# Earlier release of the projection weight pool, two more gate-row buffers, and output weights on ScalarE's DMA queue, in a hybrid Fourier and state-space layer

## The chip, the core and the metric

The kernel runs on one core of one Trainium2 chip, in one launch. The metric is the time of that launch in device microseconds (us). A core has a matrix engine (TensorE, PE in the profile; PEld is its loading of weights), a vector engine (VectorE, DVE), a scalar engine (ScalarE, ACT), a general engine (GpSimd, POOL), and SyncE (SP), which here only issues DMAs. Each engine executes its instructions in the order in which they were written for it, and waits at an instruction until the semaphores that it names are reached.

## The reference, cut to what matters

One layer works on 2048 latent tokens and 256 context tokens of width 1024, all in fp32:

```
u, zf, zs, xbc, dt_raw = split(h @ w_in)       # h: modulated, normalised tokens
mixed = real(fft2(u)) over (2048 positions, 64 channels of a group)
four  = (mixed @ w_fourier + b_fourier) * silu(zf)          # 512 channels
xbc   = silu(depthwise_conv3x3(xbc) + b)                    # x 1536, B 512, C 512
y     = ssd_scan_forward(...) + ssd_scan_backward(...) + d_skip * x
ssd   = group_rmsnorm(y * silu(zs)) * norm_w                # 1536 channels
out   = final_rmsnorm(x + gate * (concat(four, ssd) @ w_out))
```

The scan works in 16 chunks of 128 positions (and 2 of context), 4 groups of 6 heads, in both directions.

## The kernel before, in words

Matrix products are made in three passes over a high and a low part of each operand (`hh`/`hl` are the high and low part of the tokens, `wh`/`wl` those of a weight tile; L176, L177 and L178 are the three passes of a projection). The stages are, by the profile: normalisation, the `u` projection and the first DFT; the projection and convolution of 20 channel tiles; then the backward scan, interleaved with the `zs` projection (the gate) of token blocks 0 to 2; then the `zs` projection of token block 3, interleaved with the rest of the Fourier branch; then 64 output units of one chunk and group each, which read everything back from DRAM.

**Projection weights.** `weights` (L163) fills a tile in a chain: one DMA of 512 KB to the single buffer `raw` (SP's queue), a copy to `wh` on ACT (L68), and the subtraction that gives `wl` on POOL (L72). `raw` can be loaded again when `wl` is done. `wh` and `wl` have two buffers each. The pool that holds them is `p1w`; it is closed after the first two units' first step (L1090).

**The `zs` block 3 and the Fourier branch.** `interleave` (L756) writes twelve tiles of the projection (tiles 19 to 8, of 24 matmuls each) and puts the steps of a side list between them by their estimated cost: `f_table` (L905; PE at L909), `f_step2` (L916; PE at L923), `f_extra` (L982), and `f_mm` (L962; PE at L941 to L943). `f_mm` is called for four channel tiles `dt`, two halves of the positions `h` and two parts `i`; each call has 12 matmuls. After its second part `f_gate` (L945) adds the bias, and multiplies into the gate rows `zf` (L960), which `zf_load` (L896) has fetched, 1 MB for each `dt`. After the second half of a `dt` the product is stored to DRAM (`fm_d<-zf`). There are two `zf` buffers, so the third and fourth `dt` wait at `zf_load` for the store of the first and second. `interleave` hands back what did not fit (`left`), which is written behind the projection (L1043).

**The units.** Step `s1` of a unit loads its rows `rt`, `lt` (small), `cb`, `chl`, `yb`, `zs`, `xg`, `bt`. PE makes the arguments of the decay (L1079), DVE masks them (L1081), ACT takes the exponential (L1083), PE multiplies (L1115 to L1117, L1136 to L1138, L1151, L1154), the norm follows (L1167), and the output product (L1210 to L1212) reads the output weights `wo`.

**The output weights.** They are 32 pieces of 512 KB (`hl<-wo_d`, `hh<-wo_d`), which `w_load` (L853) puts into the places of the tokens as these come free, in four groups of 8 loads. Group 1 is written in the side list before the last `f_mm` calls, group 0 behind the last projection tile (L1042), and groups 2 and 3 in the units 0 and 1 behind `issue_after`, which holds a group until named instructions have gone.

**What sets the order.** The program is written for all engines together; a scheduler then simulates it and fixes one order for each engine. Every DMA of this kernel is issued on SP's queue. The DMAs take eight semaphores in turn, and a DMA is only issued when the DMA before it on its semaphore has landed.

Of the kernel before, what the change touches and what calls it, by code (L numbers as in the profile page):

```python
# [9 lines left out]
F32 = mybir.dt.float32  # L10
# [8 lines left out]
P = 128  # L19
# [30 lines left out]
def mixer_layer(ctx: ExitStack, tc: tile.TileContext, A: dict, out: bass.AP, taps=None):  # L50
# [798 lines left out]
    wos = {}  # L849
# [3 lines left out]
    def w_load(n):  # L853
        r, k = 2 * (n % 4), worder[n]
        wos[k] = tuple(t[:, r:r + 2, c:c + 512] for t, c in wplace[n // 4])
        for i in range(2):
            load(wos[k][i].bitcast(F32), wo_d[k, :, i].rearrange("p (a b) -> p a b", a=2).bitcast(F32))
# [7 lines left out]
    fa = pool("fa", 2, stack=pfa)  # L865
    fb = pool("fb", 2, stack=pfb, side="right")
    c64 = [const_tile("c64", where=fa), const_tile("s64", where=fa)]
# [4 lines left out]
    fo = {"new": main_psum}  # L872
    gls = {}
# [22 lines left out]
    def zf_load(dt):  # L896
        def go():
            zf = zft[dt] = fb.tile([P, 16, P], F32, name="zf", tag="zf")
            load(zf[:].rearrange("p a b -> p (a b)"), zfT_d[dt])
            if dt != 2:  # L900
                nc.scalar.activation(zf, zf, AF.Silu)
            nc.gpsimd.tensor_tensor(out=zf[:, :, 64], in0=zf[:, :, 64], in1=ye[:, dt], op=ALU.mult)
        return go
# [41 lines left out]
    def f_gate(dt, p0, p1, parts):  # L945
        zf = zft[dt]
        q32 = fb.tile([P, 512], F32, name="q32", tag="q32", bufs=1)
        copy(q32, p1)
# [59 lines left out]
    dts = [0, 3, 1, 2]  # L1008
# [8 lines left out]
    fmm = [(dt, h) for dt in dts[:2] for h in range(2)] + [(dt, h) for h in range(2) for dt in dts[2:]]  # L1017
    for n, (dt, h) in enumerate(fmm):
        if n in (4, 5):
            side.append((0.0, zf_load(dt)))  # L1020
        if n == 6:
            side.append((0.0, lambda: w_group(1)))
        side += [(2.6, f_mm(dt, h, i)) for i in range(2)]
    left = interleave(zs_ops([(i, (3,)) for i in range(19, 7, -1)]), side, 10, .75)
# [16 lines left out]

    w_group(0)  # L1042
    for _, fn in left:  # L1043
        fn()
# [45 lines left out]
    p1w.close()  # L1090
# [157 lines left out]
    for u in range(NU + 2):  # L1248
        if u + 1 < NU:
            if u > 0:  # L1250
                s1(u + 1)
            s2(u + 1)
        if u < 2:
            with tc.issue_after(fo["st"]), tc.issue_after(units[u + 1]["ld"]):
                w_group(u + 2)
        if u < NU:
            s3(u)
            s4(u)
        if 1 <= u <= NU:
            s5(u - 1)  # L1260
        if u >= 2:
            s6(u - 2)
# [110 lines left out]
```

## Time and profile before

| what | value |
| --- | --- |
| median of 3 runs | 1911.37 us (1909.71 to 1916.48) |
| the profiled execution | 1912.61 us |
| its span from the first to the last instruction | 1910.8 us |
| mean granted TensorE clock | 0.977 of full speed |
| PE busy | 1809.4 us, 95% of the span |
| DVE, ACT, POOL busy | 66%, 46%, 47% |
| data moved by DMA | 301.80 MB, 158 GB/s in the mean |

A row of the timeline gives the start and the length of an instruction, its engine and line, what it writes and reads, and in brackets how long the engine stood idle before it and what released it. The chain of waits is followed back from the last instruction; each row is one piece of it. A row of the windows gives the busy time and the number of instructions of PE, PEld, DVE, ACT and POOL in a stretch of time, then the granted TensorE clock, the busy share of the DMA engines, and the GB/s moved. An issue on SP's queue is written `SPq`; its length is that of the issue, not of the transfer.

### The profile page before, as it was taken

The page shows a single profiled execution, that of the slowest core. Times are in us where ns is not written, and L with a number is a line of the kernel's source. Part 1 is how long each engine was busy: PE and PEld are TensorE (multiplying, and loading weights), DVE is VectorE, ACT ScalarE, POOL GpSimd, SP SyncE. Part 2 cuts the span into 40 slices and gives each one's busy share as a digit, 9 for nine tenths or more (in the row PEclk, how much of TensorE's full clock was granted, in tenths as well). Part 3 has the DMA queues.
Part 4 walks back from the last instruction along what each step waited for, and adds up shares of the span by engine and source line. Part 5 has one row for each costly group of instructions (what it writes and reads, how often), then busy time and mean ns, then how long its engine had stood idle before and what let it go on. Part 6 is the DMA issues. An engine that isn't in the chain of part 4 may idle for free.

```text
span 1910.8 us, 28132 instructions
## 1 busy us (share of the span) xinstructions
PE 1809.4 (95%) x9142; PEld 1492.4 (78%) x9142; DVE 1258.5 (66%) x1809; ACT 873.9 (46%) x1968; POOL 906.2 (47%) x791
## 2 busy tenths in 40 slices
PE   6989999999999999989999999957999999999997
PEld 2779988888888888878888877845778777777776
DVE  3744569788888897557665622334677777667865
ACT  3632235445445455346666653223444444435443
POOL 1320034224123134178787732145777777668742
PEclk8999999999999999999999999977999999999999
DMA  7432344535445345367776774786445444444441
GB/s 256 166 93 77 90 131 151 171 113 166 138 130 160 122 129 174 120 200 217 213 218 206 216 247 136 224 287 218 125 143 151 130 132 134 147 124 138 144 137 44
DMA packets 291332, 301.80 MB, mean 158 GB/s; under 512 B 34098, under 2 KB 242066, under 8 KB 290675
## 3 DMA queue, kind: packets, MB, share of 16 engines
q1 hardware_dynamic: 291186, 300.01, 50.6%
q8 instruction: 73, 1.20, 0.3%
q14 instruction: 73, 0.59, 0.1%
HBM read 196.82 MB, written 103.10 MB: 157 GB/s over the span
## 4 chain that ended last, share of the span: by engine, by line
PE 75%; DMA 9%; DVE 5%; POOL 5%; issue 3%; ACT 2%; SPq 1%; POOLq 0%; DVEq 0%; ACTq 0%
PE pj L178 11%; PE pj L177 11%; PE pj L176 11%; PE po L1212 6%; PE po L1210 6%; PE po L1211 6%; PE py L1151 2%; PE parg L1079 2%; POOL sl L72 2%; PE pj L508 1%; PE pj L509 1%; PE pj L510 1%; PE py L1154 1%; DMA ev<-in_wout 1%; PE ptr L569 1%
## 5 line engine op out<-in xcount | busy, mean ns | idle before, releaser
L178 PE MATMUL pj<-hh,wl 128*128 128x512 f32 x1152 | 452.6, 393 | 0.8 <-POOL wl L72 0.8
L177 PE MATMUL pj<-hl,wh 128*128 128x512 f32 x1152 | 452.1, 392 | 0.0
L176 PE MATMUL pj<-hh,wh 128*128 128x512 f32 x1152 | 450.0, 394 | 2.1 <-ACT img L68 1.6
L636 DVE SCALAR_TENSOR_TENSOR pacc<-img,c_convw,pacc 128x1024 f32<-128x1024 f32 x320 | 410.0, 1287 | 58.5 <-ACT pacc L633 49.2
L72 POOL TENSOR_TENSOR wl<-raw,wh 128x1024 fp32r<-128x1024 f32 x48 | 116.5, 2428 | 345.4 <-ACT wh L68 294.8
L178 PEld LDWEIGHTS pj<-hh,wl 128*128 128x128 f32 x1152 | 216.4, 188 | 47.4 <-POOL wl L72 1.4
L176 PEld LDWEIGHTS pj<-hh,wh 128*128 128x128 f32 x1152 | 217.0, 188 | 44.4 <-ACT img L68 2.3
L177 PEld LDWEIGHTS pj<-hl,wh 128*128 128x128 f32 x1152 | 216.6, 188 | 40.9 <-issue 1.8
L807 ACT ACTIVATE xd<-xt,smb 128x64 f32<-128x64 f32 x384 | 100.8, 336 | 80.2 <-POOL yb L811 78.5
L1210 PE MATMUL po<-hl,mh 128*128 128x512 f32 x288 | 117.5, 408 | 0.7 <-ACT mh L68 0.4
L1211 PE MATMUL po<-hh,mh 128*128 128x512 f32 x288 | 114.8, 399 | 0.0
L1081 DVE COPY_PREDICATED parg<-msk,parg 128x384 f32<-128x384 uint8 x128 | 71.1, 556 | 64.1 <-PE parg L1079 63.7
L1212 PE MATMUL po<-hl,ml 128*128 128x512 f32 x288 | 109.8, 401 | 2.6 <-POOL ml L72 2.4
L1083 ACT ACTIVATE w<-parg 128x384 f32<-128x384 f32 x128 | 62.3, 486 | 104.8 <-DVE parg L1081 104.5
L72 DVE TENSOR_TENSOR xl<-xw,xh 128x384 fp32r<-128x384 f32 x76 | 63.7, 843 | 59.3 <-ACT xh L68 57.9
L1120 POOL TENSOR_TENSOR ts<-ts,yb 128x384 f32<-128x384 f32 x64 | 73.6, 1150 | 57.6 <-issue 27.2
L1079 PE MATMUL parg<-rt,lt 128*128 128x384 f32 x256 | 88.0, 372 | 11.2 <-DMA rt<-cum_d 4.1
L72 POOL TENSOR_TENSOR ml<-gt,mh 128x384 fp32r<-128x384 f32 x64 | 68.4, 1068 | 58.8 <-ACT mh L68 55.4
L68 ACT ACTIVATE xh<-xw 128x384 fp32r<-128x384 f32 x136 | 69.9, 516 | 55.2 <-PE pst L1138 14.9
L1084 DVE TENSOR_TENSOR w<-w,cb 128x768 f32<-128x768 f32 x64 | 81.6, 1275 | 12.1 <-ACT w L1083 10.9
L72 DVE TENSOR_TENSOR sl<-hbk,sh 128x384 fp32r<-128x384 f32 x64 | 59.9, 937 | 38.4 <-ACT sh L68 38.2
L72 POOL TENSOR_TENSOR sl<-ev,sh 128x512 fp32r<-128x512 f32 x32 | 42.1, 1317 | 89.1 <-DMA wo_d<-sl 38.3
(388 smaller groups left out, 4132.7 us busy)
## 6 DMA issues: line engine op xcount, KB each, us to landing
raw<-in_win SPq DMA_DIRECT2D x48, 512.0 KB
xt<-xtok_d SPq DMA_DIRECT2D x80, 192.0 KB
xtok_d<-tk SPq DMA_DIRECT2D x48, 256.0 KB
zsT_d<-ev SPq DMA_DIRECT2D x48, 256.0 KB
yb_d<-yb SPq DMA_DIRECT2D x64, 192.0 KB
yb<-yb_d SPq DMA_DIRECT2D x64, 192.0 KB
zs<-zsT_d SPq DMA_DIRECT2D x64, 192.0 KB
xg<-xtok_d SPq DMA_DIRECT2D x64, 192.0 KB
```

The source lines that it names most:

```text
L72: (lo_engine or nc.vector).tensor_tensor(out=lo, in0=src, in1=hi.bitcast(F32), op=ALU.subtract)
L176: mm(po, wh[:, k], a, start=(k == 0), stop=False)
L177: mm(po, wh[:, k], b, start=False, stop=False)
L178: done["mm"] = mm(po, wl[:, k], a, start=False, stop=(k == KT - 1)).ins
L636: nc.vector.scalar_tensor_tensor(out=acc, in0=im[:, r0 + dy:r0 + dy + 16, dx:dx + GRID_W], scalar=tap(t), in1=acc, op0=ALU.mult, op1=ALU.add)
L807: nc.scalar.activation(xd[:, h], d["x"][:, h], AF.Copy, scale=smb[:, 3, c, g * HG + h:g * HG + h + 1])
L1079: mm(po, l[:, dr], r[:, cols], start=True, stop=True)
L1084: nc.vector.tensor_tensor(out=w, in0=w, in1=cb[:].unsqueeze(1).broadcast_to([P, HG, P]), op=ALU.mult)
L1120: nc.gpsimd.tensor_tensor(out=ts, in0=ts, in1=yb, op=ALU.add)
L1210: mm(po, a, wh[:, i], start=(g == 0 and q == 0), stop=False)
L1211: mm(po, a, wl[:, i], start=False, stop=False)
L1212: mm(po, b, wh[:, i], start=False, stop=(g == 3 and q == 3))
```

## The change

Four things change together:

- `w_load` issues the output weights on ScalarE's queue (`nc.scalar.dma_start`) in place of SP's.
- `p1w` is closed before the pool `fb` of the Fourier branch is opened, which now takes its place. The projection weights of block 3 come from a new pool `wp2` of the same shape, beside `fb`. It is closed behind the last projection tile, and a pool `fz` is opened in its place, with two more `zf` buffers for the third and fourth `dt`.
- The order of the `dt` is 0, 1, 3, 2 in place of 0, 3, 1, 2. All of `f_mm` for the first two is interleaved with the projection, and that for the other two is written behind it.
- Group 0 of the output weights is written behind the projection as before; group 1 follows the first half of the last two `dt`, and groups 2 and 3 the second half, each behind the last copy `q32` of `f_gate` on ACT. The groups 2 and 3 in the units 0 and 1 are gone.

```diff
@@ w_load
-            load(wos[k][i].bitcast(F32), wo_d[k, :, i].rearrange("p (a b) -> p a b", a=2).bitcast(F32))
+            nc.scalar.dma_start(out=wos[k][i].bitcast(F32),
+                                in_=wo_d[k, :, i].rearrange("p (a b) -> p a b", a=2).bitcast(F32))
+
+    def w_after(g):
+        with tc.issue_after(fo["q"]):
+            w_group(g)
...
     fa = pool("fa", 2, stack=pfa)
+    p1w.close()
     fb = pool("fb", 2, stack=pfb, side="right")
+    p2w = ctx.enter_context(ExitStack())
+    W["p"] = pool("wp2", 2, stack=p2w, side="right")
...
+    fz = {"p": fb}
...
-            zf = zft[dt] = fb.tile([P, 16, P], F32, name="zf", tag="zf")
+            zf = zft[dt] = fz["p"].tile([P, 16, P], F32, name="zf", tag="zf")
...
-        copy(q32, p1)
+        fo["q"] = copy(q32, p1)
...
-    dts = [0, 3, 1, 2]
+    dts = [0, 1, 3, 2]
...
-    fmm = [(dt, h) for dt in dts[:2] for h in range(2)] + [(dt, h) for h in range(2) for dt in dts[2:]]
-    for n, (dt, h) in enumerate(fmm):
-        if n in (4, 5):
-            side.append((0.0, zf_load(dt)))
-        if n == 6:
-            side.append((0.0, lambda: w_group(1)))
-        side += [(2.6, f_mm(dt, h, i)) for i in range(2)]
-    left = interleave(zs_ops([(i, (3,)) for i in range(19, 7, -1)]), side, 10, .75)
+    for dt in dts[:2]:
+        side += [(2.6, f_mm(dt, h, i)) for h in range(2) for i in range(2)]
+    interleave(zs_ops([(i, (3,)) for i in range(19, 7, -1)]), side, 10, 1, True)
+    p2w.close()
+    fz["p"] = pool("fz", 2, stack=pfb, side="right")
...
+    for dt in dts[2:]:
+        zf_load(dt)()
     w_group(0)
-    for _, fn in left:
-        fn()
+    for h in range(2):
+        for dt in dts[2:]:
+            for i in range(2):
+                f_mm(dt, h, i)()
+        if h == 0:
+            w_after(1)
+    w_after(2)
+    w_after(3)
...
     pfb.close()
-    p1w.close()
...
-        if u < 2:
-            with tc.issue_after(fo["st"]), tc.issue_after(units[u + 1]["ld"]):
-                w_group(u + 2)
```

The scheduler moves more than the diff says. Three places matter below.

**SP at the end of the scan.** `yb_d<-yb` are the last stores of the scan, `c_c` to `c_bf` small constants, `gl` and `tw` operands of the Fourier branch. Before (one more `raw<-in_win` stands fourteen rows higher, between scan loads):

```order
L63 DMA raw<-in_win 128x1024
L63 DMA yb_d<-yb_10425 128x384
L63 DMA zsT_d<-ev 128x4x128
L63 DMA c_c_10453<-in_c 128x128
L63 DMA c_s_10455<-in_s 128x128
L63 DMA c_tw_10457<-in_tw 128x32
L63 DMA c_bf<-in_bf 128x4
L63 DMA gl<-in_wf 128x512 x4
L63 DMA tw<-in_tw 128x512
L63 DMA gl<-g_d 128x512
L63 DMA zsT_d<-ev 128x4x128
```

Now:

```order
L63 DMA yb_d<-yb_10425 128x384
L63 DMA c_bf<-in_bf 128x4
L63 DMA zf<-zfT_d 128x2048 x2
L63 DMA c_c_10457<-in_c 128x128
L63 DMA c_s_10459<-in_s 128x128
L63 DMA c_tw_10461<-in_tw 128x32
L63 DMA gl<-in_wf 128x512 x4
L63 DMA tw<-in_tw 128x512
L63 DMA gl<-g_d 128x512
L63 DMA raw<-in_win 128x1024
```

The first weight tile of block 3 is now loaded behind the whole scan, and behind the two `zf` loads and the other operands of the Fourier branch, which stood behind it before.

**PE at the same place.** L802 to L804 are the scan's last product, L932 and L940 are `f_step2` (L923 and its neighbour before). Now:

```order
L802 MATMUL pj<-sh_10417,cc_10365 128x384
L803 MATMUL pj<-sl_10418,cc_10365 128x384
L804 MATMUL pj<-sh_10417,cc_10365 128x384
L932 MATMUL ptr<-tw,gl 128x128 x4
L940 MATMUL ptr<-c_tw_10461,gl 128x32
L176 MATMUL pj<-hh,wh 128x512
L177 MATMUL pj<-hl,wh 128x512
L932 MATMUL ptr<-tw,gl 128x128 x4
L940 MATMUL ptr<-c_tw_10461,gl 128x32
L178 MATMUL pj<-hh,wl 128x512
```

Before, the scan's last product was followed by 42 projection matmuls of block 3 and then by the first `f_table` product; now it is followed by work on the newly loaded operands. It is the 4591st row on PE, where it was the 4597th: six projection matmuls that stood ahead of it now come behind it.

**ACT at the end of the Fourier branch.** `q` are the copies `q32` of `f_gate`, L1083 (now L1097) is the exponential of the first unit. Before:

```order
L901 ACTIVATE zf<-zf 128x2048
L131 ACT_TABLE_LOAD
L68 ACTIVATE q_11392<-pj 128x512
L68 ACTIVATE sh_11554<-hf 128x384
L68 ACTIVATE sh_11573<-hf 128x384
L68 ACTIVATE xh_11592<-xw_11590 128x384
L68 ACTIVATE q_11435<-pj 128x512
L68 ACTIVATE q_11470<-pj 128x512
L1083 ACTIVATE w<-parg 128x384
```

Now:

```order
L857 DMA hl<-wo_d 128x2x512 x6
L910 ACTIVATE zf<-zf 128x2048
L857 DMA hl<-wo_d 128x2x512 x2
L131 ACT_TABLE_LOAD
L68 ACTIVATE q_11443<-pj 128x512
L68 ACTIVATE q_11478<-pj 128x512
L857 DMA hl<-wo_d 128x2x512
...
L857 DMA hh<-wo_d 128x2x512 x9
L1097 ACTIVATE w<-parg 128x384
L68 ACTIVATE sh_11578<-hf 128x384
L68 ACTIVATE sh_11597<-hf 128x384
```

The 16 loads of groups 2 and 3 (six of them in the rows left out) stand on ACT between the last `q` and the first exponential; the copies `sh` and `xh` of the first units, which stood ahead of the last two `q`, now stand behind the exponential.

## The prediction

> **What bounds the kernel now.** I read the page's first part, then the windows, then PE's timeline where the windows fall, then what holds PE there.
>
> ```profile
> PE 1809.4 (95%) x9142; PEld 1492.4 (78%) x9142; DVE 1258.5 (66%) x1809; ACT 873.9 (46%) x1968; POOL 906.2 (47%) x791
> ```
>
> PE is the bound: its work is the same in both kernels, so only its idle time and its clock can change. 1910.8 - 1809.4 = 101 us are idle. The windows show where:
>
> ```profile
> 1090.00:1110.00 20.00, 20.00 (x94) 17.08 (x94) 11.29 (x17) 14.78 (x47) 11.46 (x10) 1.00 0.66 210
> 1110.00:1130.00 20.00, 19.36 (x77) 14.08 (x76) 2.63 (x4) 4.82 (x8) 5.83 (x4) 1.00 0.76 241
> 1240.00:1260.00 20.00, 10.85 (x49) 8.74 (x47) 2.23 (x4) 4.37 (x7) 8.00 (x9) 0.84 1.06 366
> 1260.00:1280.00 20.00, 9.27 (x44) 7.30 (x44) 13.47 (x20) 5.31 (x12) 12.32 (x12) 0.59 0.67 202
> 1280.00:1300.00 20.00, 13.03 (x52) 9.43 (x48) 6.83 (x14) 4.68 (x11) 6.39 (x6) 0.67 0.90 311
> 1300.00:1320.00 20.00, 12.03 (x54) 9.48 (x54) 7.30 (x11) 4.63 (x11) 8.79 (x9) 0.71 0.70 227
> 1320.00:1340.00 20.00, 19.01 (x101) 15.64 (x100) 11.48 (x21) 8.09 (x19) 14.92 (x16) 1.00 0.54 153
> ```
>
> The change touches two passages. From the scan to block 3 (1090 to 1130) PE is full. From the Fourier branch to the units (1250 to 1313) it idles, and what it does runs on half a clock or little more. PE's timeline of that passage:
>
> ```profile
> 1250.34 0.51 PE L1079 MATMUL parg<-rt,lt 128*128 128x384 f32 x2
> 1267.32 0.66 PE L1115 MATMUL pyo<-sh,chl 128*128 128x384 f32 x1 [16.47 <-DVE yy L951]
> 1281.57 0.80 PE L1210 MATMUL po<-hl,mh 128*128 128x512 f32 x1 [0.40 <-ACT mh L68]
> 1289.52 0.66 PE L1079 MATMUL parg<-rt,lt 128*128 128x384 f32 x2 [2.08 <-DMA lt<-q_d]
> 1290.87 0.56 PE L1115 MATMUL pyo<-sh,chl 128*128 128x384 f32 x1 [0.69 <-DMA chl<-chl_d]
> 1305.82 1.01 PE L1079 MATMUL parg<-rt,lt 128*128 128x384 f32 x2 [4.09 <-DMA rt<-cum_d]
> 1308.69 0.69 PE L1115 MATMUL pyo<-sh,chl 128*128 128x384 f32 x1 [1.85 <-DMA chl<-chl_d]
> 1312.70 0.42 PE L1115 MATMUL pyo<-sh,chl 128*128 128x384 f32 x1 [1.08 <-DMA chl<-chl_d]
> 1313.30 0.39 PE L1210 MATMUL po<-hl,fm 128*128 128x512 f32 x1
> ```
>
> The last `f_mm` ends where the first row begins; call that moment T. `DVE yy` is only the last link of the 16.47 us. Behind it are the fourth gate row, and ACT's and SP's queues:
>
> ```profile
> 1240.97 8.29 SPq L63 DMA_DIRECT2D hl<-wo_d  x8
> 1249.31 1.23 SPq L63 DMA_DIRECT2D zf<-zfT_d  x1
> ...
> 1278.05 0.26 SPq L63 DMA_DIRECT2D rt<-cum_d  x1
> 1279.35 0.28 SPq L63 DMA_DIRECT2D lt<-q_d  x1
> ```
>
> ```profile
> 1249.31 12.74 DMA zf<-zfT_d
> ```
>
> ```profile
> 1264.98 0.60 ACT L68 ACTIVATE q<-pj 128x512 f32<-128x512 f32 x1 [19.23 <-DVE yy L951]
> 1268.94 0.49 ACT L1083 ACTIVATE w<-parg 128x384 f32<-128x384 f32 x1 [3.37 <-DVE parg L1081]
> ```
>
> The fourth `zf` is issued behind eight output-weight loads and lands at about 1262; the gate chain runs; the first exponential starts at 1268.94, T + 18.6. From then to the product with `fm` at 1313.30 it takes another 44.4 us, of which 2.08 + 0.69 + 4.09 + 1.85 + 1.08 = 9.8 are waits for inputs of the next units, issued from 1278.05 on.
>
> **The change part by part.** *Passage 1, the pool that moves.* The loads ahead of the first `raw` are the cost. SP and PE before:
>
> ```profile
> 1112.80 0.33 SPq L63 DMA_DIRECT2D raw<-in_win  x1
> 1113.76 0.32 SPq L63 DMA_DIRECT2D yb_d<-yb  x1
> 1116.16 0.37 SPq L63 DMA_DIRECT2D zsT_d<-ev  x1
> 1116.63 0.46 SPq L63 DMA_DIRECT2D c_c<-in_c  x1
> ...
> 1118.60 1.86 SPq L63 DMA_DIRECT2D gl<-in_wf  x4
> ```
>
> ```profile
> 1110.13 0.39 PE L176 MATMUL pj<-hh,wh 128*128 128x512 f32 x1
> 1110.36 0.39 PE L177 MATMUL pj<-hl,wh 128*128 128x512 f32 x1
> ...
> 1110.81 0.34 PE L803 MATMUL pj<-sl,cc 128*128 128x384 f32 x1
> 1110.99 0.34 PE L804 MATMUL pj<-sh,cc 128*128 128x384 f32 x1
> ```
>
> ```profile
> 1121.54 1.10 PE L909 MATMUL pj<-gl,c_c 128*128 128x512 f32 x2 [0.65 <-DMA gl<-in_wf]
> ```
>
> The scan's last product ends at 1111.3. Ahead of it six projection matmuls drop out, at the pitch of 0.23 us at which the first two rows start: PE runs out at about 1109.9. Before, 10 us of projection (42 matmuls) followed with a gap of only 0.65.
>
> After: the last `yb_d` follows the last product by 2.4 us as before (1113.76 against 1111.3), so about 1112.3. Behind it twelve issues go before `raw` (bf, two zf, three constants, four wf, tw, gl), at the 0.46 us of the rows above: 5.5 us, `raw` at 1117.8 if none waits. But issues share eight semaphores: the tenth (the last wf) and the eleventh (tw) wait for the second and third, the two zf. These and the wf ahead of them are some 2.9 MB, at the 366 GB/s of the window at 1240 7.9 us from the first zf's issue at 1112.8: tw goes at about 1121, `raw` at 1122. I take 1122, since the eight semaphores are seen at work in passage 2. From `raw`'s issue to `wl`:
>
> ```profile
> 1142.86 5.14 DMA raw<-in_win
> 1148.08 1.07 ACT wh L68
> 1149.22 2.38 POOL wl L72
> ...
> 1172.84 0.89 PE ptr L923 x8
> ```
>
> 8.7 us at the longest of that row, and some 7 with less beside it; PE's first two passes can begin 2.4 sooner, and then stand at L178. So PE works from about 1129 in earnest: 19 us after it ran out. It has little instead of it: the first step2 rows, 0.89 us each (two of them stand there). Behind such a gap the clock is half for a while, as in the windows at 1260 and 1280; a dense 4 us at half cost 2 us. Off that go the 0.65 us of gap that PE had there, 1.8 of the two step2, and 1 to 2 for L176 and L177 ahead of `wl`: 19 + 2 - 0.65 - 1.8 - 1.5 = **+17 us**. Low bound +12 (`raw` at 1118, nothing waits); high +22 (`raw` at 1123, the clock at half for 4 us and a second stop at the next tile, for `raw` has one buffer). The later tiles keep up: 12 tiles of this 8 us chain are 96 us, and PE has 24 x 12 x 0.23 = 66 us of projection and the tables, step2 and f_mm, 139 us in all from 1111 to 1250.
>
> *Passage 2, the zf wait.* With four `zf` buffers the third and fourth are loaded behind the first stores and ahead of the last 30 us of f_mm (eleven calls of 12 matmuls now stand behind the last projection, nine before). The 12.74 us row goes. The gate chain then ends some 3 us behind T. If that were all, the first exponential would come at T + 8, 10.6 sooner: before, it came 6.7 us after `zf` had landed (1262.2 to 1268.94), and the last `q` comes about 1 us behind T.
>
> *What is late next: the 16 loads on ACT.* They stand between the last `q` and the exponential. An issue is 0.46 us, so 16 x 0.46 = 7.4: T + 8 if none waits. But by the eight semaphores the last can only go when the eighth has landed, and the two `fm_d` stores on SP are in the same rotation: 8 x 0.524 + 2 x 1.05 = 6.3 MB, at 366 GB/s 17 us, plus about 2 to land. So exponential at **T + 19.5**; from the other side 16 x 0.524 + 2.1 = 10.5 MB, 28.7 us, T + 29. Behind that exponential on ACT are the copies `sh` and `xh`, for which PE's L1115 and L1136 wait: PE stands. I take T + 19.5 against T + 18.6 before: +1.
>
> The Trainium skill, "DMA: Bandwidth & Descriptors", section "Issuing engines are not separate DMA queues", says that DMAs of ScalarE, SyncE and GpSimd run on the same 16 engines, and that a second issuer saves only issue time. By it the move alone buys nothing but the 0.46 us each on SP, which is what I count.
>
> *Behind the exponential.* The weights of groups 2 and 3 are under way while PE stands, not between the loads of units 2 and 3. Before, eight of them went at 1289.98 and held the rows behind, at 0.67 and 0.71 of the clock. I count the 9.8 us of waits as gone, and of the slow clock from 1292 to 1312 some 4 us (the windows at 0.67 and 0.71): -14. Bounds: 0, if the loads of units 2 and 3 still queue behind the same bytes; -16.
>
> ```profile
> 1289.98 5.64 SPq L63 DMA_DIRECT2D hh<-wo_d  x8
> ```
>
> *Order of dt, step `q`.* No work changes; PE's 12 matmuls per call are the same.
>
> The sum: 17 + 1 - 14 = +4. The profiled execution was 1912.61 us, 1.2 above the median, so about 1916.6 for such an execution and **1915** against the median.
>
> **The rivals.**
>
> *A, slower: the loads hold ACT until they have nearly all landed.* If the semaphores are so taken that the 16th waits for most of the 10.5 MB, the exponential starts at T + 29, and passage 2 is +10.4 - 14 = -4. With +17: 1924. It decides from T + 25 on. For it: SP's issues from 1278.05 came one per 1.3 us, which is a 512 KB load at full rate; against it: in the 30 us of f_mm ahead of T only groups 0 and 1 and two zf are to be moved (10.5 MB, 29 us at 366 GB/s), so most semaphores should be free at T.
>
> *B, slower: the bytes, not the queue.* Units 2 and 3 still find their small loads behind megabytes; the 14 us are not saved: 1911.4 + 17 + 1 = 1929. For it: the windows at 1280 and 1300 show 311 and 227 GB/s, and the same 16.8 MB must move. Against it: 1256 to 1260 moves 409 GB/s with PE idle, room that the loads can take.
>
> ```profile
> 1256.00:1260.00 4.00, 0.00 (x0) 0.00 (x0) 0.00 (x0) 0.00 (x0) 0.00 (x0) 0.50 1.04 409
> ```
>
> The page named above speaks for it: packets of all queues are served in turn on the same engines.
>
> *C, faster: ACT is not held.* The issues take 7.4 us, the exponential starts at T + 8, passage 2 saves 10.6 + 14 = 24.6; with +17 it is 1911.4 - 7.6 = 1904, and with passage 1 at its low bound 1899. For it: ACT needs nothing else there, and the waits may be on loads long done. Against it: 16 loads of 1.4 us each cannot land in 7.4.
>
> *D: passage 1 at its low bound alone* (`raw` not held, +12): 1910.
>
> **How the numbers follow.** The forecast 1915 with its own range 1903 to 1922: 0.42. A 0.18, B 0.13, C 0.17, D 0.10. A difference of 0.5% is 9.6 us, about what a measurement can tell from none: faster is below 1901.8, slower above 1920.9. Faster: half of C and a fourth of D, and 0.06 of the forecast's case where both terms lean down: 0.09 + 0.02 + 0.06 = 0.17. Slower: nearly all of A (0.15) and B (0.13), and a few hundredths of the forecast: 0.32. Same: 0.51. The range of 8 in 10 reaches to C's lower end and to B: 1898 to 1930.
>
> **What the profile would show.** Passage 1: a PE gap of 15 to 20 us from about 1110, released by ACT `wh` or POOL `wl`, with `raw` issued at 1118 to 1122 behind the zf loads; a gap under 10 makes the first term wrong, and then the time is 1907 or less. Passage 2: no wait for `zf` on DVE; ACT issuing output weights from about T to T + 19; first exponential near T + 19.5; no waits of PE for `rt`, `lt`, `chl` up to the `fm` product, which follows T by about 50 in place of 63. If ACT is done at T + 8, C is right; if PE still waits for unit inputs for 10 us, B. A time below 1898 would mean that block 3's weights came in time after all.

## The result, and the profile after

The changed kernel takes 1931.58 us (median of four runs, 1928.47 to 1933.87) against 1911.62 us before (1909.71 to 1916.48): a ratio of 1.0103, with a 95% interval of 1.0089 to 1.0118. It is slower by 20 us, 1.6 us beyond the upper end of the range. The profiled execution, the slowest of the four, took 1933.87 us, its span 1932.1 us.

The windows of the changed kernel (PE, PEld, DVE, ACT and POOL busy, then granted clock, DMA share, GB/s):

```profile
1090.00:1130.00 40.00, 22.86 (x107) 19.43 (x106) 14.01 (x22) 20.36 (x57) 11.39 (x12) 0.84 0.75 242
1240.00:1260.00 20.00, 20.00 (x90) 16.57 (x89) 6.59 (x9) 2.88 (x5) 2.58 (x2) 1.00 1.02 327
1260.00:1280.00 20.00, 11.34 (x49) 8.87 (x47) 9.80 (x13) 4.51 (x5) 7.13 (x7) 0.86 1.02 374
1280.00:1300.00 20.00, 2.03 (x5) 1.55 (x6) 0.74 (x2) 2.22 (x5) 1.59 (x2) 0.50 1.06 357
1300.00:1320.00 20.00, 13.16 (x60) 10.10 (x60) 9.46 (x17) 6.35 (x15) 14.31 (x15) 0.70 0.78 270
1320.00:1340.00 20.00, 18.78 (x106) 14.73 (x104) 13.86 (x22) 8.74 (x21) 14.88 (x15) 1.00 0.41 125
```

Both passages show. Between 1090 and 1130 PE now works 22.9 us of 40, where it was full. And the DMA engines are full from 1240 to 1300, while PE stands almost still from 1280 to 1300. PE's timeline of the changed kernel:

```profile
1129.39 2.05 PE L932 MATMUL ptr<-tw,gl 128*128 128x128 f32 x8 [17.14 <-DMA gl<-g_d]
...
1270.14 0.51 PE L1093 MATMUL parg<-rt,lt 128*128 128x384 f32 x2
1279.02 0.69 PE L1093 MATMUL parg<-rt,lt 128*128 128x384 f32 x1 [8.37 <-DVE parg L1095]
1297.97 0.69 PE L1093 MATMUL parg<-rt,lt 128*128 128x384 f32 x1 [18.26 <-ACT w L1097]
...
1327.24 0.48 PE L1223 MATMUL po<-hl,fm 128*128 128x512 f32 x1
```

The gap of 17.14 us is the first passage. T, the end of the last `f_mm`, is 1270.1 in place of 1250.3. Behind it PE waits 8.37 us for the gate chain on DVE and 18.26 us for the first exponential. ACT, with its DMA issues (`ACTq`), says why:

```profile
1274.79 0.60 ACT L68 ACTIVATE q<-pj 128x512 f32<-128x512 f32 x1 [1.63 <-DVE yy L960]
1274.82 0.37 ACTq L857 DMA_DIRECT2D hl<-wo_d  x1
...
1278.50 0.37 ACTq L857 DMA_DIRECT2D hh<-wo_d  x1
1290.47 0.37 ACTq L857 DMA_DIRECT2D hl<-wo_d  x1
1290.87 6.51 ACTq L857 DMA_DIRECT2D hh<-wo_d  x9
1297.43 0.49 ACT L1097 ACTIVATE w<-parg 128x384 f32<-128x384 f32 x1 [22.04 <-DMA hh<-wo_d]
```

Six of the 16 loads go within 4 us, the seventh only 12 us later, the rest in 6.5 us; the exponential starts at 1297.43, T + 27.3. What the seventh waits for can be followed by the semaphores in the trace: it takes the semaphore of the first of the two stores that SP issues beside the row,

```profile
1276.10 7.26 SPq L63 DMA_DIRECT2D fm_d<-zf  x2
```

and that store landed at 1290.44. The second store held the row up to 1293.46, and two of its last loads took the semaphores of its seventh and eighth, which landed at 1295.11 and 1296.46. When the exponential starts, eight of the 16 loads have landed, not all.

Since the first 1110 us vary from one execution to the next (below), executions are compared in pieces. S is the start of the scan's last product, T the end of the last `f_mm`, both from PE's timeline; the last piece reaches from T to the end of the span. "exp" is the start of the first exponential.

| kernel | S | S to T | exp - T | T to the end | span |
| --- | --- | --- | --- | --- | --- |
| before | 1111.0 | 139.4 | 18.6 | 660.5 | 1910.8 |
| changed | 1111.9 | 158.2 | 27.3 | 661.9 | 1932.1 |

So the loss of 21.3 us is, but for rounding, 0.9 + 18.8 + 1.4: the first passage costs 18.8 us, and behind T, where a gain of 13 was forecast, nothing is won by the end.

The last piece holds more than the second passage: all 64 units are in it, and the scheduler writes them in another order for almost every kernel, however small the edit. So the progress behind T is also counted in matmuls. Every kernel has 3253 of them from T to the end, some 5.4 per us where PE is busy throughout (1615 in the 300 us from T + 200 of the kernel before). The counts are the PE column of a window that starts at T:

| kernel | by T + 200 | by T + 500 | by T + 600 |
| --- | --- | --- | --- |
| before | 842 | 2455 | 3001 |
| changed | 862 | 2477 | 2994 |
| e4 | 906 | 2515 | 3056 |
| e6 | 888 | 2498 | 3029 |
| e9 | 882 | 2497 | 3042 |
| e13 | 929 | 2532 | 3076 |

By T + 200 the changed kernel is 20 matmuls ahead, some 4 us, and by the end it has lost them again. (e4 to e13 are runs of the next section.)

### The profile page after: what moved, and what is told of

It is laid out like the page before. It is cut to its first block, busy times and chain, and to the rows that moved or that the text cites. A ratio compares the mean times of both kernels' runs of the same rounds, so it can differ in the third digit from the quotient of the medians.

```text
span 1932.1 us, 28125 instructions
## 1 busy us (share of the span) xinstructions
PE 1812.1 (94%) x9142; PEld 1494.9 (77%) x9142; DVE 1257.0 (65%) x1809; ACT 873.9 (45%) x1968; POOL 906.8 (47%) x791
## 4 chain that ended last, share of the span: by engine, by line
PE 44%; DMA 6%; POOL 5%; DVE 3%; issue 3%; ACT 2%; SPq 1%; ACTq 0%; POOLq 0%; DVEq 0%
PE po L1225 6%; PE po L1224 5%; PE po L1223 5%; PE pj L177 4%; PE pj L178 4%; PE pj L176 4%; PE py L1164 2%; PE parg L1093 2%; PE py L1167 1%; DMA xt<-xtok_d 1%; DMA zf<-zfT_d 1%; POOL sl L72 1%; POOL yb L811 1%; DMA fm_d<-zf 1%; PE ptr L932 1%
## 5 line engine op out<-in xcount | busy, mean ns | idle before, releaser
L1097 ACT ACTIVATE w<-parg 128x384 f32<-128x384 f32 x128 | 62.4, 487 | 120.1 <-DVE parg L1095 97.5
L72 POOL TENSOR_TENSOR sl<-hf,sh 128x384 fp32r<-128x384 f32 x64 | 73.3, 1146 | 50.4 <-ACT sh L68 50.2
```

The lines of the kernel that those rows point to most:

```text
L72: (lo_engine or nc.vector).tensor_tensor(out=lo, in0=src, in1=hi.bitcast(F32), op=ALU.subtract)
```

## The experiments

All kernels but e13 were timed several times beside the kernel before; the ratio is to the kernel before. The pieces are read as above, from one profiled execution each. The expectations of e9, e10 and e11 count T to the end from a point some 9 us later: their 653 and 638 us are the 661.9 and 646.7 of the changed kernel and e4 here, and their 642 seems to be the 651.2 of e7.

| run | what differs | median, us | ratio (95%) | S to T | exp - T | T to the end |
| --- | --- | --- | --- | --- | --- | --- |
| e1 | change, first `raw` ahead of zf and wf | 1935.66 | 1.0108 (1.0078 to 1.0138) | 156.3 | 31.9 | 663.3 |
| e2 | change, old pools | 1931.07 | 1.0087 (1.0066 to 1.0108) | 139.0 | 45.6 | 675.5 |
| e3 | change, 16 loads behind four exponentials | 1930.65 | 1.0085 (1.0060 to 1.0110) | 158.8 | 8.7 | 657.9 |
| e4 | change, all output weights on SP | 1918.10 | 1.0026 (1.0013 to 1.0038) | 159.5 | 4.7 | 646.7 |
| e5 | before, output weights on ACT | 1917.09 | 1.0027 (1.0013 to 1.0041) | 139.5 | 26.2 | 664.7 |
| e6 | before, group 1 behind the fourth zf | 1911.78 | 0.9990 (0.9975 to 1.0004) | 139.3 | 8.6 | 659.8 |
| e7 | change, weights on SP and spread as before | 1925.15 | 1.0068 (1.0047 to 1.0088) | 159.0 | 5.2 | 651.2 |
| e8 | before, only the order of dt and f_mm | 1923.07 | 1.0051 (1.0036 to 1.0066) | 139.4 | 23.9 | 666.7 |
| e9 | change, groups 2 and 3 alone on SP | 1918.51 | 1.0030 (1.0020 to 1.0040) | 158.2 | 7.5 | 649.4 |
| e10 | before, groups 2 and 3 in one row | 1919.33 | 1.0044 (1.0027 to 1.0062) | 140.5 | 18.3 | 663.0 |
| e11 | e6 and e10 together | 1914.35 | 1.0003 (0.9989 to 1.0017) | 140.2 | 8.0 | 663.3 |
| e12 | change, old pools, weights on SP behind zf | 1922.58 | 1.0049 (1.0032 to 1.0066) | 139.5 | 15.3 | 670.5 |
| e13 | change, half the bytes of groups 2 and 3 | 1920.71 (one execution) | | 157.3 | 22.1 | 648.8 |
| e14 | e6, and group 3 behind unit 3's inputs | 1909.88 | 0.9979 (0.9967 to 0.9991) | 140.3 | 7.8 | 659.7 |

### Passage 1: the pool or the order of the loads (e1, e2)

e1 puts the first weight tile ahead on SP:

```diff
+    zw["next"] = weights(19)
+    raw1 = W["ld"]
     for j in range(4):
         wfs.append(gl_tile())
-        load(wfs[j], A["wf"][j])
+        with tc.issue_after(raw1):
+            load(wfs[j], A["wf"][j])
...
-            side += [(0.0, zf_load(dt)) for dt in dts[:2]]
+            side += [(0.0, zf_behind(dt)) for dt in dts[:2]]     # zf_load within issue_after(raw1)
```

> The changed kernel, with the first weight tile of block 3 (raw) put ahead of the two zf loads and the four wf loads in SP's order; the pools are the changed ones. Theory 1 (the 17 us gap of PE at the end of the scan is raw standing behind those loads): raw is issued some 9 us sooner (1114 to 1115 in place of 1123.5), PE's gap falls from 17 to 6 to 9 us, and the time from 1931.6 to about 1921 to 1923. Rival (the gap is the pool change as such, PE would wait for the Fourier operands or for the clock anyway): the gap stays above 14 us and the time above 1928.

PE's timeline of e1:

```profile
1123.54 0.79 PE L176 MATMUL pj<-hh,wh 128*128 128x512 f32 x1 [9.16 <-ACT wh L68]
1126.02 0.79 PE L178 MATMUL pj<-hh,wl 128*128 128x512 f32 x1 [1.26 <-POOL wl L72]
1137.14 1.99 PE L932 MATMUL ptr<-tw,gl 128*128 128x128 f32 x8 [2.73 <-DVE xe L942]
```

Neither theory held; only the time lies on the rival's side. The gap does shrink, from 17.14 to 9.16 us, but `raw` was issued at 1118.5, only 5 us sooner, with four constants still ahead of it and a scan that ended 2 us later; and the operands put behind it are late next (1.26 and 2.73 us). From S to T it is 156.3 us against 158.2: 2 us won, and nothing in the time. In these two orders, what comes second in that place has no work to cover it.

e2 takes back the pools alone (two `zf` buffers again, the third and fourth waiting for the stores):

```diff
-    p1w.close()
     fb = pool("fb", 2, stack=pfb, side="right")
-    p2w = ctx.enter_context(ExitStack())
-    W["p"] = pool("wp2", 2, stack=p2w, side="right")
...
-    p2w.close()
-    fz["p"] = pool("fz", 2, stack=pfb, side="right")
...
     pfb.close()
+    p1w.close()
```

> The changed kernel with the pools of the kernel before: the projection weights of block 3 stay in the old pool, there are two zf buffers, and the third and fourth zf wait for the stores of the first and second. The order of the dt, the position of the output weights and ScalarE's queue are as in the change. Theory 1 (all of the 19.8 us by which the Fourier branch ends later is the moved pool): the gap at the scan's end is gone, the last f_mm ends near 1250; the zf wait costs 0 to 5 us, since the first two dt are stored 14 us or more ahead of the end; ACT is still held by the loads for some 27 us. Time 1911 to 1918. Rival (the pool is not the cause): above 1925.

S to T is back at 139.0 us: the moved pool is the whole of the 18.8 us. In all eight runs with the old pools (e2, e5, e6, e8, e10, e11, e12, e14) that piece is 139.0 to 140.5, in all six with the new ones (e1, e3, e4, e7, e9, e13) 156.3 to 159.5. But the time did not fall, and lies where the rival had it, since T to the end went from 661.9 to 675.5. ACT and SP of e2, of the fourth gate row and of the first exponential:

```profile
1263.52 0.32 SPq L63 DMA_DIRECT2D zf<-zfT_d  x1
```

```profile
1287.55 12.39 ACTq L857 DMA_DIRECT2D hh<-wo_d  x9
1299.99 0.49 ACT L1092 ACTIVATE w<-parg 128x384 f32<-128x384 f32 x1 [27.51 <-DMA yb<-yb_d]
```

Here T is 1254.4, yet the exponential comes at 1300, as late as in the changed kernel, where T was 1270. It starts right behind the row's last issue; the `yb` in its brackets is nothing that it reads. The fourth `zf` now waits again, for the second store, and with it the last `q` and the 16 loads behind that.

### Passage 2: who holds whom (e3, e4, e9, e5)

e3 lets the first four exponentials go ahead of the loads on ACT:

```diff
-    w_after(2)
-    w_after(3)
...
     for u in range(2):
         s1(u)
+    with tc.issue_after(units[1]["exp"]):
+        w_group(2)
+        w_group(3)
```

> The changed kernel with the 16 output-weight loads of groups 2 and 3 behind the first four exponentials on ScalarE, in place of ahead of them. Theory 1 (ACT is held by the loads' semaphores from T + 5 to T + 27, and the hold only moves): the first exponential starts at T + 8 to T + 10, but ACT is held behind the fourth exponential until T + 27 or later, PE does the two units' matmuls that need no more of ACT and then stands; 1921 to 1929. Rival (with the first exponentials out, the hold is covered): 1913 to 1917. Second rival (the DMA traffic sets the time, whoever waits): 1930 or more.

PE's timeline of e3, where the units stop:

```profile
1317.47 0.69 PE L1091 MATMUL parg<-rt,lt 128*128 128x384 f32 x1 [25.72 <-ACT w L1095]
```

The hold only moved, as theory 1 has it: the first exponential starts at T + 8.7, and then PE stands 25.7 us for the fifth. From T to the end 657.9 us against 661.9; its median of 1930.65, a little above theory 1's range and in the second rival's, cannot be told from the changed kernel's. So e3 alone does not exclude that rival (the DMA traffic, whoever waits); e4, with the same bytes, does.

e4 issues the output weights on SP again; it is the only edit to the changed kernel, though the scheduler's order of the later units differs with it:

```diff
-            nc.scalar.dma_start(out=wos[k][i].bitcast(F32), in_=...)
+            load(wos[k][i].bitcast(F32), ...)
```

> The changed kernel with all output-weight loads issued on SP's queue again. Theory 1 (an issuer that takes these loads is held until most have landed, whichever it is): ACT is free and the first exponential starts at T + 8 to T + 10, but SP is held to about T + 28, the fm_d stores and the inputs of units 2 and 3 come behind it, and the product with fm follows T by 57 or more as before; 1920 to 1932. Rival (ScalarE's hold was the whole loss of this passage): the product with fm follows T by 40 to 45, 1913 to 1919.

1918.10 us, 13.5 below the changed kernel: by its time in the rival's range. Of theory 1's picture SP's hold (the last load goes at 1300.6, T + 29.8) and the mark are right, of the rival's the time. PE's timeline of e4:

```profile
1275.01 0.44 PE L1092 MATMUL parg<-rt,lt 128*128 128x384 f32 x1 [3.74 <-DVE parg L1094]
...
1307.42 1.07 PE L1092 MATMUL parg<-rt,lt 128*128 128x384 f32 x2 [20.24 <-DMA lt<-q_d]
```

and its windows:

```profile
1250.00:1270.00 20.00, 20.00 (x90) 16.57 (x89) 8.29 (x13) 5.00 (x5) 4.64 (x5) 1.00 1.06 380
1270.00:1290.00 20.00, 9.91 (x54) 7.11 (x52) 11.73 (x17) 5.67 (x12) 17.75 (x17) 0.81 1.06 378
1290.00:1310.00 20.00, 1.63 (x4) 1.13 (x5) 1.27 (x3) 1.78 (x5) 0.00 (x0) 0.50 0.90 290
1310.00:1330.00 20.00, 16.48 (x67) 13.32 (x66) 10.75 (x20) 7.15 (x17) 15.50 (x15) 0.75 0.59 188
```

The DMA engines are as full as in the changed kernel (1.06), and the product with `fm` follows T by the same 57 us. But the stop comes elsewhere. SP is held now, so units 0 and 1, whose inputs are already there, are worked off (9.91 us of PE between 1270 and 1290) before PE stands 20.24 us for unit 2's `lt`. With ACT held, PE stands before unit 0, with everything it needs in place. From T to the end that is 646.7 us against 661.9: the queue costs 15.2 us. By T + 200 e4 is 44 matmuls ahead of the changed kernel, some 8 us, and 38 ahead by T + 500; so about half of the 15.2 us lies in the passage, and the rest comes in the last 160 us, which these runs do not explain (the other order of the units is one possible reason). Against the kernel before, 646.7 is 13.8 us less, and 64 matmuls more by T + 200, some 12 us: the gain that was forecast for this passage is there, and the queue takes it away. That is what the rival says; its mark, the product with `fm` at T + 40 to 45, was wrong, as below.

e9 keeps groups 0 and 1 on ScalarE's queue and gives 2 and 3 to SP:

```diff
+        eng = nc.scalar if n < 8 else nc.sync
-            nc.scalar.dma_start(...)
+            eng.dma_start(...)
```

> The changed kernel with groups 0 and 1 of the output weights on ScalarE's queue and groups 2 and 3 on SP's. Theory 3 (what costs on ScalarE's queue is only the row of 16 loads ahead of the first exponential; T to the end was 653 us with all on ACT, 638 with all on SP): first exponential at T + 5 to T + 9, T to the end 636 to 642, time 1916 to 1921. Rival (the loads of group 1 ahead of the zf activation hold the gate as well): 1924 to 1930.

1918.51 us, as e4, and 649.4 us from T, which is what theory 3 expects with those 9 us added. So in the time only the row of 16 loads ahead of the exponential costs; the 16 of groups 0 and 1, which ACT issues while PE has `f_mm` to do, cost nothing that shows. By T + 200, though, e9 is only 20 matmuls ahead of the changed kernel, where e4 is 44: here too a good part comes later.

e5 makes the other half: the queue alone, in the kernel before.

> The kernel before with one edit: the output weights are issued on ScalarE's queue. Pools, zf buffers, order of dt are those before. The 16 loads of groups 2 and 3 then come on ACT ahead of the last q and the first exponential. Theory 2 (the queue that takes the 16 loads in one row is held until most have landed, and the units start behind that, whatever else is done): first exponential at 1295 to 1302 in place of 1269, time 1922 to 1932. Rival (the queue is harmless, the loss of the change is the moved pool): 1908 to 1916.

Neither fits. The time is 1917.09, 4.6 us slower, and the exponential starts at 1281.4, not at 1295 or later. The 16 loads begin there some 16 us sooner than in the changed kernel, at 1258.5, ahead of the last `q`, and so are through sooner:

```profile
1258.52 0.37 ACTq L857 DMA_DIRECT2D hh<-wo_d  x1
...
1275.66 1.72 ACTq L857 DMA_DIRECT2D hh<-wo_d  x2
1277.48 0.60 ACT L68 ACTIVATE q<-pj 128x512 f32<-128x512 f32 x1 [17.38 <-DMA hh<-wo_d]
```

The queue costs by what stands behind the row at that moment: 15 us in the changed kernel, 4 to 5 here, where the fourth `zf` is late anyway.

### Bytes or semaphores (e13)

The changed kernel, with `wos[k][i][:, :1]` in place of the whole piece for groups 2 and 3.

> The changed kernel with half of each of the 16 loads of groups 2 and 3 left out (256 KB in place of 512 KB; the same number of DMAs on ScalarE's queue; the other half of these output weights is not loaded, so the product is made with other numbers). Theory 3 (ACT is held by the bytes that must land, 0.385 MB per us): the first exponential comes 8 to 11 us sooner, at T + 16 to T + 19. Rival (the eight semaphores hold it behind the DMAs ahead, the zf rows, group 1 and the stores, or the issues themselves): at T + 24 or later.

ACT of e13:

```profile
1278.32 0.33 ACTq L858 DMA_DIRECT2D hh<-wo_d  x1
1286.40 0.33 ACTq L858 DMA_DIRECT2D hl<-wo_d  x1
1286.77 5.39 ACTq L858 DMA_DIRECT2D hh<-wo_d  x9
1292.20 0.49 ACT L1098 ACTIVATE w<-parg 128x384 f32<-128x384 f32 x1 [18.03 <-DMA hh<-wo_d]
```

The exponential starts at T + 22.1, between the two expectations: 4.2 MB fewer (10.9 us at 0.385 MB per us) bring 5.2 us. The stop ahead of the seventh load falls from 11.6 to 7.8 us and stays. If the other half is worth as much, some 10 of the 22 us for which ACT waits belong to the row itself; the rest belongs to what was under way when the row began (group 1, the `zf` rows, the two stores). The semaphores fit this. The seventh load, at 1286.40, again takes that of the first `fm_d` store, which landed at 1286.38. Theory 3 counted the bytes of all 16 loads, but only eight have to land before the exponential: half of these is 2.1 MB, 5.4 us at 0.385 MB per us, against 5.2 measured.

The run shows one thing more: from T to the end it takes 648.8 us, 13.1 less than the changed kernel and nearly as little as e4, with the loads still on ScalarE's queue. What the queue costs is thus a matter of its bytes too. This is one execution of a kernel that computes other numbers.

### What the other parts are worth (e7, e8, e10, e12)

e7 is the changed kernel with the weights on SP, and groups 2 and 3 back in units 0 and 1.

> The changed kernel with the output weights on SP's queue, and groups 2 and 3 back in the units 0 and 1 as before: what is left of the change is the moved pool, the four zf buffers and the order of the dt. Theory 2: T at 1270, no zf wait, the first exponential at T + 8 to T + 10 and the product with fm some 44 us behind it as before, that is 1321 to 1324; 1916 to 1923. Rival (the loss at the scan is hidden anyway, since the bytes set the start of the units): 1909 to 1914.

1925.15, 2 us above theory 2's range; from T to the end 651.2. So with the four `zf` buffers, and all on SP, one row of 16 (e4, 646.7) is 4.5 us better than the spread (7 us in the medians): of the 14 us that I counted for moving these loads forward, a third to a half is real. The spread with four buffers is in turn 9.3 us better than the kernel before (660.5): that is what the buffers and the new order bring together.

e8 takes from the change the order of the `dt` and of the `f_mm` calls alone.

> The kernel before with only the order of the dt (0, 1, 3, 2) and of the f_mm calls of the change (the first two dt wholly between the projection tiles, the other two behind it); pools, queue and position of groups 2 and 3 as before. Theory 2: the fourth zf load is still behind eight loads and the second store; first exponential within 5 us of before; 1908 to 1917. Rival (the order alone lets the stores go early enough that the wait is gone): 1900 to 1907.

Neither fits: 1923.07, slower than before. The two stores and the two `zf` loads then follow one another at the end of the `f_mm` calls; SP of e8:

```profile
1247.43 0.43 SPq L63 DMA_DIRECT2D zf<-zfT_d  x1
1247.97 0.37 SPq L63 DMA_DIRECT2D fm_d<-zf  x1
1248.44 11.21 SPq L63 DMA_DIRECT2D hl<-wo_d  x8
1259.90 0.84 SPq L63 DMA_DIRECT2D zf<-zfT_d  x1
```

The fourth `zf` goes at 1259.9, behind the second store and eight loads: T + 5.1, where it was T - 1.0 before. Without the spare buffers the new order costs 11 us in the median; it depends on them.

e10 and e12 put the weights in one row with two `zf` buffers, in the old order and in the new.

> The kernel before with one edit: groups 2 and 3 are written right behind the last f_mm, on SP's queue, in place of in the units 0 and 1. Theory 3 (loads in one row ahead of the unit inputs cost no more than loads between them, since the DMA engines are full either way: 638 us from T to the end against 642): the zf wait and the first exponential as before (T + 18 to T + 20), time within 6 us of before, 1906 to 1918. Rival (SP held by the row is as bad as ACT held): 1922 or more.

> The changed kernel with the pools of before (two zf buffers), all output weights on SP's queue, and groups 1 to 3 behind the fourth zf load. It differs from the run with the old pools alone (1931) in the queue and in that order. Theory 3: no gap at the scan's end (T at 1252 to 1256), the fourth zf still waits for the second store, first exponential at T + 10 to T + 16, time 1903 to 1911. Rival (without the spare zf buffers the order of the dt costs as in the run of the order alone, 1923): 1918 or more.

1919.33 and 1922.58 us. e10 lies just above the range, between its theories: with the old order the row costs 6 us in the median. e12 falls on its rival's side: its exponential comes at T + 15.3 as I expected, but 670.5 us from T to the end is the worst but one, for the units stand behind the row from there. These runs do not say why the row is harmless with four buffers and not with two.

### The wait of the kernel before, by itself (e6, e11, e14)

e6 leaves everything as before but for the place of group 1 on SP:

```diff
-            side.append((0.0, lambda: w_group(1)))
+            side.append((0.0, w_behind_zf))       # w_group(1) within issue_after(the fourth zf load)
```

> The kernel before with one edit: the eight loads of group 1 stand behind the fourth zf load on SP, not ahead of it. All on SP's queue, pools as before. Theory 2 (the 16.5 us wait before was the zf row behind eight loads): the zf row lands some 8 to 10 us sooner, first exponential at 1258 to 1262, and since the later loads are still spread between the units, 1902 to 1908. Rival (the bytes set the end, group 1 only comes later): 1910 to 1915.

PE's timeline of e6:

```profile
1259.18 0.66 PE L1120 MATMUL pyo<-sh,chl 128*128 128x384 f32 x1 [6.44 <-DVE yy L951]
...
1284.61 0.66 PE L1084 MATMUL parg<-rt,lt 128*128 128x384 f32 x2 [2.69 <-DMA lt<-q_d]
...
1303.37 0.98 PE L1084 MATMUL parg<-rt,lt 128*128 128x384 f32 x2 [9.09 <-DMA lt<-q_d]
```

By its time the rival: the 16.5 us wait shrinks to 6.4, the exponential starts at T + 8.6 in place of T + 18.6, and the time stays (ratio 0.9990). PE now waits 9.09 us for unit 3's rows, which are issued behind group 3, where it waited 4.09. But that is not where the 10 us go: by T + 200 e6 is 46 matmuls ahead of the kernel before, some 8 us, by T + 500 still 43, and only the last 160 us take them back. Why, these runs do not show; the rival's reason, the bytes behind T, is not shown by e6 either.

e11 adds the row of 16.

> The kernel before with two edits: group 1 behind the fourth zf load, and groups 2 and 3 in one row behind the last f_mm, all on SP's queue. The pools are those before, so the scan's end has no gap. Theory 3: T at 1250 to 1255 and 638 to 643 us from there to the end, as with the four zf buffers; 1899 to 1905. Rival (the bytes behind T set the start of unit 3 whatever their order, and what is saved ahead of it is given back): 1909 to 1914.

1914.35: the rival again, and here by T + 200 too, with 841 matmuls against 842 before. e14 instead sends group 3 behind unit 3's inputs (`if u in (0, 2)` in place of `if u < 2`).

> The kernel before with group 1 behind the fourth zf load, and group 3 behind the inputs of unit 3 in place of those of unit 2; all on SP's queue. Theory 3 (what the earlier exponential won there was given back where PE waited 9 us for unit 3's rows behind group 3): that wait is gone, but unit 3's product waits for group 3; T to the end 650 to 657 in place of 660, time 1902 to 1909. Rival (the bytes of the four groups set the start of unit 3 whatever their order): 1909 to 1915.

The 9 us wait is gone; the longest waits of PE in the units' start are now these:

```profile
1262.98 0.66 PE L1120 MATMUL pyo<-sh,chl 128*128 128x384 f32 x1 [5.69 <-DVE yy L951]
1295.82 0.66 PE L1120 MATMUL pyo<-sh,chl 128*128 128x384 f32 x1 [4.05 <-DMA chl<-chl_d]
```

1909.88 against 1914.11 us beside it: faster by 0.2% (0.9967 to 0.9991), the only kernel of the study whose interval lies below the kernel before. It is less than theory 3 had it: the time is at the lower end of the rival's range, and T to the end, 659.7, is not the 650 to 657 expected. Its profiled execution was the slowest of its ten (1918.23, with S at 1116.5), so its pieces do not show where it gains.

## Why the prediction was wrong, step by step

In the terms of the sum, 17 + 1 - 14, the profiled executions have 18.8, then 8.7 (the first exponential at T + 27.3 in place of T + 18.6), then -7.3 (from it to the end 634.6 us in place of 641.9), and 0.9 ahead of S.

- **Passage 1, +17: right, and a little short.** A PE gap of 15 to 20 us from about 1110 was named and is there (17.14 us), with `raw` behind the `zf` loads. SP of the changed kernel:

```profile
1114.95 0.88 SPq L63 DMA_DIRECT2D zf<-zfT_d  x2
1117.64 2.53 SPq L63 DMA_DIRECT2D gl<-in_wf  x4
1122.58 0.33 SPq L63 DMA_DIRECT2D tw<-in_tw  x1
1123.48 0.38 SPq L63 DMA_DIRECT2D raw<-in_win  x1
```

  `tw` waits for the second `zf` row as worked out (its semaphore came free at 1122.56), and `raw` goes at 1123.5 where 1122 was forecast. What ends the gap is not what I named, ACT `wh` or POOL `wl`: the first row behind it is `f_step2`, and it waits for `gl<-g_d`, issued just ahead of `raw` and landed at 1129.3. `raw` landed at 1129.7, so the two come to the same time. The piece from S to T costs 18.8 us; e2 shows that all of it is the pool.

- **The clock after the gap, 2 us: about right.** Three windows of the changed kernel:

```profile
1128.00:1132.00 4.00, 2.50 (x11) 2.40 (x12) 0.00 (x0) 1.30 (x3) 0.11 (x1) 0.50 0.55 208
1132.00:1136.00 4.00, 4.00 (x18) 3.46 (x19) 1.47 (x5) 1.36 (x6) 2.26 (x1) 0.68 0.42 110
1136.00:1140.00 4.00, 4.00 (x20) 3.29 (x19) 0.42 (x1) 1.07 (x2) 0.87 (x1) 1.00 0.44 157
```

  Dense work has the full clock again 4 to 6 us after it starts. The Trainium skill, "TensorE: Matmul & The Clock Gate", section "What's actually happening", gives one window of about 3.4 us of sustained work for that, at half rate. Here it took some 5 us: PE starts at 1129.39, and 0.68 in the second window is half rate for 2.6 of its 4 us. That is 2.6 us lost.

- **The zf wait goes: right but for some us.** Where nothing holds ACT (e4, e7), the exponential starts at T + 4.7 and T + 5.2, where T + 8 was forecast. In the changed kernel the last `q` comes at T + 4.7 in place of T + 1: the `zf` rows were issued late and run beside group 1. SP's and ACT's issues of the changed kernel:

```profile
1256.77 3.72 SPq L63 DMA_DIRECT2D zf<-zfT_d  x2
```

```profile
1259.54 4.80 ACTq L857 DMA_DIRECT2D hl<-wo_d  x6
...
1266.51 4.73 ACTq L857 DMA_DIRECT2D hl<-wo_d  x2
```

- **"The 16 loads on ACT", T + 19.5: the step that failed.** It was T + 27.3. I let the row of 16 begin with free semaphores and counted 6.3 MB from T on; against rival A I wrote that groups 0 and 1 and two `zf` rows would be moved in the 30 us ahead of T. They were not: group 1, which waits for the `q` of the first half, was issued from 1259.5 to 1271.2, that is T - 10.6 to T + 1.1, and seven of its eight loads landed only from T + 1.6 to T + 9.7, one per 1.35 us. The rest of the step held: from there to the landing of the row's eighth load, 8 loads and 2 stores or 6.3 MB as counted, it took 16.6 us where 17 were forecast. So the term that I put at nothing, the backlog at T, measures 9.7 us and belonged into the sum. Rival A's T + 29 is the nearer number by luck: it had nearly all 16 loads land first, and eight had. Its price of 1924 was too low for the next reason.

- **"Behind the exponential", -14: the mark was wrong.** From the exponential to the product with `fm` it is 29.8 us in place of 44.4, which is 14.6 less. But that product is not the same place in the work: before, it stood behind the norms of three units, now behind those of two. Unit 2's norm product starts at T + 66.5, and started at T + 50.6. The 9.8 us of waits for inputs are gone as forecast (one of 0.84 us is left ahead of that product), but unit 2's rows `rt` are issued no sooner from T, 28.5 us against 27.7:

```profile
1298.69 0.86 SPq L63 DMA_DIRECT2D rt<-cum_d  x2
```

  They wait last for PE: its argument product of unit 0 (1297.97 to 1298.66) reads the buffer that `rt` fills, and has itself waited for the first exponential. The semaphore that `rt` takes had come free 0.7 us sooner, at 1297.97. So ACT's hold reaches the next units too. Counted to the end 1.4 us are lost behind T, and by T + 200 some 4 us are won, where a gain of 13 was forecast. As a mark I should have taken a product of the same unit, or a count of matmuls.

- **The queue, counted at its issue time: wrong.** I took from the Trainium skill, "DMA: Bandwidth & Descriptors", section "Issuing engines are not separate DMA queues", that a second issuer saves issue time and no more. The runs agree with that for the transfers (the DMA engines are full at 1.06 on either queue), but the price was on the other side. The same page of the Trainium skill, section "Anatomy of one DMA — SWDGE (gpsimd) path", says that a wait on a semaphore is made by the issuing sequencer before it dispatches. That is what the ACT rows show (the seventh load, and all behind it on ACT, stand 11.6 us for a store's landing), and e4 prices: 15.2 us from T to the end, 13.5 us in the median. Without the queue the change would have come to 1918.1, 3 us from the forecast.

- **Rival B** (the bytes, not the queue) named a time of 1929, the nearest of all, by another way: units 2 and 3 do find their inputs behind the same megabytes (e4, e6), but with the weights on SP, and the same bytes, T to the end is 13.8 us shorter than before, so the bytes alone did not decide. They are not innocent either: what ACT waited for was bytes that had to land, and half of those of groups 2 and 3 brought 13.1 us (e13).

## What to carry to other kernels

A DMA that has to wait for a semaphore holds the engine that issues it, and everything behind it there (here ACT, for 11.6 us at one load). Put bulk loads on an engine whose next instructions are not wanted soon, and count the backlog that is already under way when the row begins, not only the row's own bytes. When a pool is moved to free memory for one stage, look at what it loaded ahead across the border of the stage before: here that prefetch was worth 19 us, more than the 14 by which everything behind T became shorter at best (e4). And measure a passage between two points with the same work ahead of both; a piece that reaches to the end of the kernel also holds what the scheduler does there.

## What was not expected of the hardware

The first 1110 us, which no edit changes much, are not equally long from one execution to the next: S lies between 1107.5 (e9) and 1116.5 (e14). The clock of the first 50 us does not explain it: it was 0.83 in the profiled executions before and of e14 (S at 1111.0 and 1116.5), and 1.00 in those of the changed kernel and e9 (1111.9 and 1107.5). These 9 us are half of what the change cost; the cause is open, and single spans of this kernel can't be compared more finely than that.
